# Row mathematics turned on TensorE, merged weight transfers and rows of x for the second block in a pooling and mLSTM layer

## The chip, the core and the metric

The program runs on one core of a Trainium2 chip. The metric is the device time of one execution in microseconds, median of three runs. The engines are named as the profile names them: PE (TensorE), DVE (VectorE), ACT (ScalarE), POOL (GpSimd) and SP (SyncE, whose queue issues all DMAs here).

## What is computed

One layer over x of 2048 tokens with 1024 features: an RMS norm, one input projection, two branches (pooling, and an mLSTM in both directions), a gated merge and an output projection with a second norm.

```python
def hybrid_layer(x, norm_pre_g, w_in, ...):
    h = rms_norm(x, norm_pre_g)          # x * rsqrt(mean(x*x) + EPS) * g
    proj = jnp.einsum('bsd,de->bse', h, w_in)
    u_a, z_a, q, k, v, o, z_b, gates, g_a, g_b = jnp.split(proj, split_points, axis=-1)
    ...                                  # pooling branch: y_a
    q, k = silu(centred_depthwise_conv([q, k])), split again
    ...                                  # gates: i_pre, f_pre, per direction and head
    h_fwd = mlstm_direction(qh, kh, vh, i_pre[0], f_pre[0])
    h_bwd = flip(mlstm_direction(flip(qh), flip(kh), flip(vh), flip(i_pre[1]), flip(f_pre[1])))
    ...                                  # norm, gates: y_b
    merged = sigmoid(g_a + b_merge[0]) * p_a + sigmoid(g_b + b_merge[1]) * p_b
    out = jnp.einsum('bsd,de->bse', merged, w_out)
    return x + rms_norm(out, norm_post_g)

def mlstm_direction(q, k, v, i_pre, f_pre):      # chunks of 128 tokens, 16 of them
    log_f = log_sigmoid(f_pre);  b = cumsum(log_f) in each chunk
    ...
    def step(carry, xs):                          # from chunk to chunk
        m_new = jnp.maximum(bl + m_st, m_add)     # bl, m_add: one number per head and chunk
        ...
```

## The kernel before

Phase 1 is the input projection, and the change lies in it. It treats the tokens in two halves of 1024, each of two blocks of 512, and the columns of w_in in 38 pairs of 128. Each factor is split into an upper part (h) and a rest (l), and a product is three matmuls, h·h, h·l, l·h (`mm3`, L107 to L109). Pairs 0 and 1 of each half are done plainly (`quarters`, L429 to L431); from pair 2 on a Strassen scheme takes sums of the two blocks (S1 to S4, from `combos`) and of the weights (T1 to T4, from `prep_w`, L355 the differences). PSUM banks A, B and C take the products; `u`, `p` and `sg` are what DVE and ACT make of the banks (L398, L403, L746), and a bank's next product waits for that.

The order of the instructions is made by a scheduler from priorities (`high_priority`) and ties (`issue_after`); each engine then runs its list in order. SP's list holds the DMAs, in order too.

**The start** (`operands`, half 0). xT comes as 8 tiles of 512 tokens for each block. For each block, `sums` squares the tiles on ACT (L243), adds the squares on DVE (L245) and sums them over partitions on PE (`ssqp`, L249). `rstd_of` takes the mean on DVE (L154) and the power on POOL (L156), `rows_of` spreads it with four matmuls (`rbp`, L178) and an ACT copy (`rb`, L185). Then DVE scales xT (L197), ACT rounds it (A11h and so on, L95), and DVE or POOL takes the rest (L99). The busy matmuls (L262) only keep PE at work. `sums(1)` is tied behind the second scaled tile of block 0. In `quarters` the order on PE is tied at the last two tiles of block 0 to `rbp` of the block after.

**The weights.** In half 0 `load_w` loads a pair as two tiles `wraw` of 512 KB, `prep_w` makes B11, B21, B22 and T1 to T4, h on ACT and l on POOL or DVE, and `keep_w` (L344) writes the T's to DRAM, h and l in a DMA each. In half 1 `again_w` reads them back (L319, L324, L336). The tiles of both parts come from the pool `wc` with 20 buffers.

**The row mathematics** (`row_math`, half 1). It works on 128 rows (direction, head, chunk) by 128 tokens. After two scans along each row (L853, L854) it takes the last column of each, `ends`, [128, 2], through DRAM (L859) and back as 4 rows of heads with 16 chunks (L864), scans over the chunks (L869), writes the result through DRAM (`carry`, L876) and reads it back as a column (L879). It is a generator: one step is taken in each of the pairs in `ROWS`. Close to it in time are `pair_v`, whose tiles `vnh` and `vnl` have buffers in turn with the conv's `acc` (L655 clears the end of `vnl`, L661 transposes v on PE as `vtr`), and the conv's output DMA `qT<-acc` (L641).

## Time and profile before

| | |
|---|---|
| Median of three runs | 2377.75 us (2377.66 to 2380.99) |
| Profiled execution, device time | 2386.15 us |
| Its span, from first to last instruction | 2384.3 us |
| Mean granted TensorE clock, share of full speed | 0.991 |
| PE busy | 2314.4 us (97%) |
| DVE, ACT, POOL busy | 1466.4 (62%), 900.0 (38%), 1138.0 (48%) us |
| DMA | 521.63 MB, 219 GB/s over the span |

The times of rows are microseconds from the span's start, in the one profiled execution. Busy time of PE says nothing of its clock: a matmul at the lower level counts as busy for twice as long. `[idle <-engine tile line]` behind an instruction is the time its engine stood idle before it, and what ended that.

### The profile page before, as it was taken

To read this page: it belongs to the slowest core of one execution; us is meant where nothing else is said; L and a number is where in the kernel's file an instruction comes from. 1 tells how busy PE (TensorE), PEld (TensorE's weight loads), DVE (VectorE), ACT (ScalarE), POOL (GpSimd) and SP (SyncE) were. 2 spreads that over 40 slices of the span, in tenths; PEclk is the share of its full clock that TensorE was granted. 3 is DMA by queue.
4 is the path that set the end of the run, shared out by engine and by line. 5 is a ranking of instruction groups with operands and counts; after the bars stand their busy time and mean duration, and the time that the engine had idled before them with its cause. 6 is when DMAs were issued, how large, how long until landed. Compare 5 with 4: busy or idle time off the path is not lost.

```text
span 2384.3 us, 35775 instructions
## 1 busy us (share of the span) xinstructions
PE 2314.4 (97%) x12569; PEld 2001.0 (84%) x12569; DVE 1466.4 (62%) x2495; ACT 900.0 (38%) x1773; POOL 1138.0 (48%) x902
## 2 busy tenths in 40 slices
PE   6899999999999989999999999999999999999998
PEld 4688888888888878888888887998989899999786
DVE  6876666677666464455666534888975333354765
ACT  4434433333343423222322333776764111121442
POOL 4655565565545334464564540554565111233775
PEclk9999999999999999999999999999999999999999
DMA  4567656566673566878777876777657546588763
GB/s 138 174 215 276 238 207 230 208 208 223 237 259 137 178 185 201 260 262 273 253 254 244 260 250 245 226 217 234 204 159 233 174 148 207 187 279 283 248 215 124
DMA packets 303011, 521.63 MB, mean 219 GB/s; under 512 B 27504, under 2 KB 138224, under 8 KB 302832
## 3 DMA queue, kind: packets, MB, share of 16 engines
q1 hardware_dynamic: 302832, 519.35, 65.1%
q8 instruction: 99, 1.62, 0.3%
q14 instruction: 80, 0.66, 0.1%
HBM read 318.45 MB, written 200.80 MB: 218 GB/s over the span
## 4 chain that ended last, share of the span: by engine, by line
PE 79%; DVE 7%; DMA 6%; issue 3%; POOL 3%; ACT 2%; SPq 1%; POOLq 0%; DVEq 0%; ACTq 0%
PE bankB L107 8%; PE bankB L108 7%; PE bankB L109 7%; PE bankA L109 5%; PE bankA L108 5%; PE bankA L107 5%; PE bankC L108 5%; PE bankC L107 5%; PE bankC L109 5%; PE num L1232 4%; PE pb L933 2%; PE pb L932 2%; PE pb L934 2%; PE paps L933 2%; PE paps L932 2%
## 5 line engine op out<-in xcount | busy, mean ns | idle before, releaser
L99 POOL TENSOR_TENSOR wB21l<-wraw,wB21h 128x512 fp32r<-128x512 f32 x76 | 106.7, 1405 | 228.3 <-ACT wB21h L95 190.7
L635 DVE SCALAR_TENSOR_TENSOR acc<-raw,conv_w,acc 128x1026 f32<-128x1026 f32 (+1 forms) x96 | 153.8, 1615 | 10.6 <-ACT acc L630 9.7
L99 POOL TENSOR_TENSOR wB22l<-wraw,wB22h 128x512 fp32r<-128x512 f32 x76 | 115.6, 1521 | 87.3 <-ACT wB22h L95 55.2
L1216 POOL TENSOR_TENSOR qs<-q,isc 128x256 f32<-128x256 f32 x120 | 91.2, 762 | 134.2 <-PE num L1232 53.0
L933 PE MATMUL pb<-oxs,w_proj_mlstmh 128*128 128x256 f32 x512 | 144.0, 281 | 0.0
L932 PE MATMUL pb<-oxs,w_proj_mlstmh 128*128 128x256 f32 x512 | 143.6, 281 | 0.0
L934 PE MATMUL pb<-oxs,w_proj_mlstml 128*128 128x256 f32 x512 | 143.4, 280 | 0.0
L933 PE MATMUL paps<-pys,w_proj_poolh 128*128 128x256 f32 x512 | 142.9, 281 | 0.2 <-POOL pys L99 0.2
L932 PE MATMUL paps<-pys,w_proj_poolh 128*128 128x256 f32 x512 | 141.4, 281 | 0.0
L934 PE MATMUL paps<-pys,w_proj_pooll 128*128 128x256 f32 x512 | 141.1, 280 | 0.0
L99 POOL TENSOR_TENSOR wB11l<-wraw,wB11h 128x512 fp32r<-128x512 f32 x72 | 106.9, 1485 | 56.0 <-ACT wB11h L95 52.8
L398 DVE TENSOR_TENSOR u<-bankB,p 128x512 f32<-128x512 f32 x76 | 52.2, 687 | 103.0 <-PE bankB L109 95.8
L107 PE MATMUL bankC<-S1h,wT1h 128*128 128x512 f32 x272 | 106.8, 393 | 3.4 <-ACT sg L746 3.4
L107 PE MATMUL bankB<-S3h,wT3h 128*128 128x512 f32 x272 | 106.8, 393 | 2.3 <-DVE u L398 2.3
L109 PE MATMUL bankB<-S2h,wT2l 128*128 128x512 f32 x272 | 106.2, 390 | 1.3 <-DVE wT2l L99 1.3
L107 PE MATMUL bankB<-A22h,wT4h 128*128 128x512 f32 x272 | 106.1, 390 | 1.3 <-DVE u L403 1.3
L108 PE MATMUL bankB<-S2l,wT2h 128*128 128x512 f32 x272 | 106.9, 393 | 0.0
L107 PE MATMUL bankA<-A12h,wB21h 128*128 128x512 f32 x272 | 106.6, 392 | 0.1
L916 POOL TENSOR_TENSOR nm<-nm,mask 128x256 f32<-128x256 f32 x64 | 61.3, 972 | 95.2 <-DMA nm<-negM 84.6
L108 PE MATMUL bankB<-S3l,wT3h 128*128 128x512 f32 x272 | 106.7, 392 | 0.0
L109 PE MATMUL bankB<-S3h,wT3l 128*128 128x512 f32 x272 | 106.6, 392 | 0.0
L108 PE MATMUL bankC<-S1l,wT1h 128*128 128x512 f32 x272 | 106.5, 392 | 0.0
(443 smaller groups left out, 7729.2 us busy)
## 6 DMA issues: line engine op xcount, KB each, us to landing
wraw<-in_w_in SPq DMA_DIRECT2D x110, 512.0 KB, 4.6
wt<-wT2h SPq DMA_DIRECT2D x34, 256.0 KB, 4.7
wt<-wT1h SPq DMA_DIRECT2D x34, 256.0 KB, 4.4
wt<-wT3h SPq DMA_DIRECT2D x34, 256.0 KB, 3.4
wt<-wT2l SPq DMA_DIRECT2D x34, 256.0 KB, 4.8
wt<-wT1l SPq DMA_DIRECT2D x34, 256.0 KB, 4.0
wt<-wT3l SPq DMA_DIRECT2D x34, 256.0 KB, 2.9
wt<-wT4h SPq DMA_DIRECT2D x34, 256.0 KB, 2.0
```

What stands on the lines that cost most here:

```text
L99: return eng.tensor_tensor(lo, x, hi.bitcast(F32), op=ALU.subtract)
L107: nc.tensor.matmul(ps, wh, xh, start=start and kt == 0, stop=False, skip_group_check=True)
L108: nc.tensor.matmul(ps, wh, xl, start=False, stop=False, skip_group_check=True)
L109: nc.tensor.matmul(ps, wl, xh, start=False, stop=stop and kt == 3, skip_group_check=True)
L398: self.read_banks.append(nc.vector.tensor_tensor(u2, bank["B"], p1, op=ALU.add))
L635: nc.vector.scalar_tensor_tensor(acc[:, :n], raw[:, tap : tap + n], self.cw[:, ct, tap : tap + 1], acc[:, :n], op0=ALU.mult, op1=ALU.add,)
L916: nc.gpsimd.tensor_tensor(t[:, d, :, :], t[:, d, :, :], mask[:, d, None, :].to_broadcast([P, 2, P]), op=ALU.add)
L932: nc.tensor.matmul(ps, wh, xh, start=i == 0, stop=False)
L933: nc.tensor.matmul(ps, wh, xl, start=False, stop=False)
L934: nc.tensor.matmul(ps, wl, xh, start=False, stop=i == n)
L1216: nc.gpsimd.tensor_tensor(qs[d], q[:, :, ck], isc[:, d, j % 2, None, :].to_broadcast([P, 2, P]), op=ALU.mult)
L1232: nc.tensor.matmul(pn, qs[d][:, kt, :], state[:, kt, :], start=kt == 0, stop=False)
```

## The change

The change has three parts.

1. **Start.** xT is stored so that two of its 128-row tiles are one DMA (4 of 512 KB for a block in place of 8 of 256 KB). For the second block of half 0 the sum of squares is taken from rows of x: 8 tiles `xs` of 128 tokens by 512 features, each squared on ACT with the sum over the row as its accumulator (`part`), one DVE add, then `rstd_of` and `rows_of` as before. ssqp and the DVE adds remain for the first block alone. On SP the rows of x stand ahead of the second block's xT. The lower halves of the first weights are made on DVE in place of POOL.
2. **Weights.** h and l of one weight are one tile [128, 2, 4, 128]; `wc` has 10 of them. `keep_w` and `again_w` move both in one DMA of 512 KB (4 in place of 8 for a pair and half). w_in is stored by blocks, so that reading a part of a pair takes runs of 2 KB.
3. **Row mathematics.** `ends` becomes two rows of 128 on one partition by two matmuls (`re`) and an ACT copy; two scans run over 64 numbers of one partition each; two matmuls (`rc`) and an ACT copy give the columns. The DMAs of `ends` and `carry` are gone; the steps are taken in pairs 3, 4, 6, 7 and 9.

```diff
-ROWS = (3, 4, 6, 7, 9, 10)
+ROWS = (3, 4, 6, 7, 9)
...
         def fetch(b):
-            for kt in range(KT):
-                t0 = half * HALF + b * BLK
-                nc.sync.dma_start(X[kt][b], a["xT"][kt, :, t0 : t0 + BLK])
+            for q in range(KT // 2):
+                nc.sync.dma_start(room[b, q], a["xT"][half * 2 + b, :, 2 * q : 2 * q + 2])
...
-            if b == 0:
-                busy(acc[:, :P], acc)
+            busy(X[7][0][:, :P], X[7][0])
...
+        def row_sums():
+
+            self.rows_read = []
+            part = pool.tile([P, 8], F32, tag="ssq", name=self.nm("part"), bufs=2)
+            tiles = []
+            for k in range(8):
+                xs = (pool.tile if k < 5 else self.wt_pool.tile)([P, BLK], F32, tag="p" if k < 5 else "wt", name=self.nm("xs"))
+                r0 = BLK + k % 4 * P
+                self.rows_read.append(nc.sync.dma_start(xs, a["x"][r0 : r0 + P, k // 4 * BLK : (k // 4 + 1) * BLK]))
+                tiles.append(xs)
+            return part, tiles
...
-                last = sums(0)
+                last = sums()
+                part, xs = row_sums()
+                with tc.issue_after(self.rows_read[3].ins):
+                    fetch(1)
...
-                if half == 0 and b == 0 and kt == 2:
-                    with tc.issue_after(scaled[1].ins):
-                        sums(1)
+                if half == 0 and b == 0 and kt == 6:
+                    with tc.issue_after(scaled[5].ins):
+                        assert not xs
+                        nc.vector.tensor_tensor(part[:, :4], part[:, :4], part[:, 4:], op=ALU.add)
+                        self.known = self.rstd_of(part[:, :4], part[:, :4], 0, 1)[0]
+                        self.rows_of(0, 1, rb[:, BLK:], psum)
...
+                if half == 0 and b == 0 and kt > 0:
+                    with tc.issue_after(self.upper.ins):
+                        for _ in range(min(2, len(xs))):
+                            k = 8 - len(xs)
+                            x = xs.pop(0)
+                            nc.scalar.activation(x, x, AF.Square, accum_out=part[:, k : k + 1])
...
+    def parts(self, wc, n):
+
+        t = wc.tile([P, 2, 4, P], F32R, tag="wc", name=self.nm(f"w{n}"))
+        return t, (t[:, 0], t[:, 1])
...
         def kept(n):
-            W[n] = tuple(wc.tile([P, 4, P], F32R, tag="wc", name=self.nm(f"w{n}{p}")) for p in "hl")
-            for p, t in enumerate(W[n]):
-                nc.sync.dma_start(
-                    t.bitcast(F32).rearrange("p k n -> p (k n)"), self.sp[f"wt{i}"][:, self.KEPT.index(n), p, :]
-                )
+            t, W[n] = self.parts(wc, n)
+            nc.sync.dma_start(
+                t.bitcast(F32).rearrange("p a k n -> p a (k n)"), self.sp[f"wt{i}"][:, self.KEPT.index(n)]
+            )
...
-            for p, t in enumerate(W[n]):
-                self.nc.sync.dma_start(self.sp[f"wt{i}"][:, k, p, :], t.bitcast(F32).rearrange("p k n -> p (k n)"))
+            self.nc.sync.dma_start(
+                self.sp[f"wt{i}"][:, k], W[n, "both"].bitcast(F32).rearrange("p a k n -> p a (k n)")
+            )
...
-                if u == 0 and kt == KT - 2 and self.half == 0:
+                if u == 0 and kt == KT - 3 and self.half == 0:
...
-            wc = es.enter_context(tc.tile_pool(name="wc", bufs=20))
+            wc = es.enter_context(tc.tile_pool(name="wc", bufs=10))
...
-                        self.plain_w(W[i], wc, raw[i], 1, "pool")
+                        self.plain_w(W[i], wc, raw[i], 1, "pool" if half else "dve")
...
-        nc.sync.dma_start(self.sp["ends"].rearrange("q r -> r q"), ends)
         yield
-        sc = T(64, NH).rearrange("h (d q c) -> h d q c", d=2, q=2)
...
+        ps = psum.tile([1, 2, P], F32, tag="tr", name="re", bufs=2)
+        for k in range(2):
+            nc.tensor.matmul(ps[:, k, :], ends[:, k : k + 1], self.ident, start=True, stop=True)
+        sc, leaves = T(2 * P, 1).rearrange("o (q r) -> o q r", q=2), one[:1, :]
+        nc.scalar.activation(sc, ps, AF.Copy)
...
+            nc.vector.tensor_tensor_scan(
+                leaves[:, row], sc[:, 0, row], sc[:, 1, row], NEG, op0=ALU.add, op1=ALU.max
+            )
...
         yield
+        ps = psum.tile([P, 2], F32, tag="tr", name="rc", bufs=2)
+        for k, row in enumerate((enters, leaves)):
+            nc.tensor.matmul(ps[:, k : k + 1], row, self.one_c[:1, :], start=True, stop=True)
         mc = T(2)
-        nc.sync.dma_start(mc, self.sp["carry"].rearrange("q r -> r q"))
-        yield
+        nc.scalar.activation(mc, ps, AF.Copy)
...
-        "xT": f(x.T).reshape(KT, P, S),
+        "xT": f(x.T.reshape(KT, P, S // BLK, BLK).transpose(2, 1, 0, 3)),
```

First place, PE in the first block of half 0. Before, the sums of the second block's squares (ssqp) stand in its row:

```order
61 L431 MATMUL bankA_528<-A12l_401,wB21h_483 128x512
62 L429 MATMUL bankB_529<-A12h_400,wB22h_487 128x512
63 L430 MATMUL bankB_529<-A12h_400,wB22l_488 128x512
64 L249 MATMUL ssqp_441<-one_c,sq_438 128x1 x4
65 L431 MATMUL bankB_529<-A12l_401,wB22h_487 128x512
```

Now, at nearly the same place, rbp of the second block (wB_57 and wB_58 are late weights, of pair 1):

```order
57 L462 MATMUL bankB_498<-A12h_401,wB_55_457 128x512
58 L463 MATMUL bankB_498<-A12l_402,wB_55_457 128x512
59 L461 MATMUL bankA_505<-A12h_401,wB_57_462 128x512
60 L461 MATMUL bankB_506<-A12h_401,wB_58_465 128x512
61 L178 MATMUL rbp_442<-ident,rstd 128x128
62 L614 MATMUL gps_513<-A11h_399,wg 32x512
```

The four ssqp are gone, and rbp, which stood at row 78 before, stands at row 61, ahead of the gates' matmuls (gps).

Second place, DVE ahead of pair 2's `u`, in pairs 2 to 4 of half 0. Before (`wt` with two sources is a difference of weights, S4l a rest of the block sums):

```order
76 L99 TENSOR_TENSOR S4l_821<-xT_307,S4h_820 128x512
77 L99 TENSOR_TENSOR S4l_821<-xT_308,S4h_820 128x512
78 L99 TENSOR_TENSOR S4l_821<-xT_310,S4h_820 128x512
79 L99 TENSOR_TENSOR S4l_821<-xT_309,S4h_820 128x512
80 L355 TENSOR_TENSOR wt_864<-wraw_836,wt_844 128x512
...
85 L355 TENSOR_TENSOR wt_985<-wraw_957,wt_965 128x512
86 L355 TENSOR_TENSOR wt_1123<-wraw_1115 128x512
87 L398 TENSOR_TENSOR u_118_913<-bankB_885,p_117_899 128x512
88 L355 TENSOR_TENSOR wt_1125<-wraw_1117,wt_1123 128x512
```

Now:

```order
66 L99 TENSOR_TENSOR S4l_798<-xT_301,S4h_797 128x512 x2
67 L387 TENSOR_TENSOR wt_836<-wraw_813,wt_820 128x512
68 L99 TENSOR_TENSOR S4l_798<-xT_303,S4h_797 128x512 x2
...
73 L387 TENSOR_TENSOR wt_946<-wraw_923,wt_930 128x512
74 L387 TENSOR_TENSOR wt_1077<-wraw_1070 128x512
75 L387 TENSOR_TENSOR wt_1079<-wraw_1072,wt_1077 128x512
76 L430 TENSOR_TENSOR u_100_879<-bankB_851,p_99_865 128x512
77 L387 TENSOR_TENSOR wt_1087<-wraw_1072,wraw_1070 128x512
```

The difference for T4 of pair 2 stands behind two S4l and no longer behind four, and pair 4's second difference (wt_1125, now wt_1079) stands ahead of u and no longer behind it.

Third place, SP in half 1 around the first step of the row mathematics. Before (`acc` is the conv's output; rows are the row mathematics'):

```order
534 L859 DMA ends<-rows 128x2x1
535 L319 DMA wT3h_7301<-wt_95 128x512
536 L319 DMA wT3l_7302<-wt_95 128x512
537 L641 DMA qT_60<-acc_7057 128x1026
538 L336 DMA wraw_7443<-in_w_in 128x4x128
539 L864 DMA rows<-ends 4x2x16
```

Now:

```order
378 L674 DMA qT_60<-acc_6609 128x1026
379 L350 DMA wT_991_6845<-wt_95 128x1024
380 L350 DMA wT_992_6847<-wt_95 128x1024
381 L674 DMA qT_60<-acc_6620 128x1026
382 L367 DMA wraw_6983<-in_w_in 128x512
383 L350 DMA wT_994_6852<-wt_95 128x1024
```

The DMAs of `ends` have gone from between them; the conv's output stands where it stood, behind the reads of the weights, which are one DMA each.

## Rows read from the trace of the kernel before

**Rows 1.** Waits of PE, whole span: releaser, us in total, times, longest.

```profile
PE ssqp L249 <- DVE sq L245: 15.5, 2, 12.3
...
PE vtr L661 <- DVE vnl L99: 7.2, 1, 7.2
```

**Rows 2.** Timeline of PE, start: start us, us, engine line op tile, [idle <-releaser].

```profile
20.74 0.50 PE L429 MATMUL bankA<-A11h,wB11h 128*128 128x512 f32 x1 [1.24 <-ACT A11h L95]
...
24.83 0.50 PE L431 MATMUL bankA<-A11l,wB11h 128*128 128x512 f32 x1 [1.95 <-DVE A11l L99]
...
40.02 1.61 PE L249 MATMUL ssqp<-one_c,sq 128*128 128x1 f32 x8 [3.20 <-DVE sq L245]
```

**Rows 3.** Windows: length; busy of PE, PEld, DVE, ACT, POOL; PEclk, DMA share, GB/s.

```profile
14.00:16.00 2.00, 2.00 (x4) 0.92 (x5) 0.16 (x1) 1.78 (x5) 1.68 (x3) 1.00 1.05 404
...
42.00:44.00 2.00, 2.00 (x6) 1.55 (x5) 0.00 (x0) 0.00 (x0) 0.93 (x1) 0.50 0.00 0
...
46.00:48.00 2.00, 2.00 (x9) 1.45 (x8) 0.00 (x0) 0.00 (x0) 0.00 (x0) 0.73 0.00 0
...
95.00:100.00 5.00, 4.86 (x14) 3.57 (x15) 3.44 (x2) 5.00 (x10) 4.75 (x4) 0.67 0.76 207
...
854.00:856.00 2.00, 2.00 (x11) 1.64 (x10) 0.00 (x0) 0.28 (x1) 0.14 (x1) 1.00 0.21 32
...
866.00:868.00 2.00, 1.54 (x7) 1.54 (x8) 1.00 (x2) 0.39 (x1) 0.00 (x0) 0.50 0.59 179
...
868.00:870.00 2.00, 2.00 (x7) 1.67 (x7) 1.53 (x6) 1.29 (x3) 0.00 (x0) 0.57 0.99 307
```

**Rows 4.** Timeline of DVE, start.

```profile
21.31 1.78 DVE L245 TENSOR_TENSOR sq<-sq,sq 128x512 f32<-128x512 f32 x1
...
34.34 2.45 DVE L197 SCALAR_TENSOR_TENSOR xT<-xT,norm_pre_g,rb 128x512 f32<-128x512 f32 x2
...
50.26 7.47 DVE L197 SCALAR_TENSOR_TENSOR xT<-xT,norm_pre_g,rb 128x512 f32<-128x512 f32 x8 [8.43 <-ACT rb L185]
...
57.65 1.78 DVE L355 TENSOR_TENSOR wt<-wraw 128x512 f32<-128x512 f32 x1
```

**Rows 5.** Instructions that write rstd, on POOL: ns min/median/max, first and last start.

```profile
L156 POOL TENSOR_TENSOR rstd<-ssq,half_c x4: 1006/1021/1484, 14.5 to 216.8; 128x4 f32<-128x4 f32 x4
```

**Rows 6.** Timeline of PE, pairs 2 and 3.

```profile
88.97 0.50 PE L109 MATMUL bankB<-S2h,wT2l 128*128 128x512 f32 x1 [1.32 <-DVE wT2l L99]
...
94.89 0.79 PE L107 MATMUL bankC<-S1h,wT1h 128*128 128x512 f32 x1 [3.37 <-ACT sg L746]
...
104.24 0.50 PE L107 MATMUL bankB<-S3h,wT3h 128*128 128x512 f32 x1 [1.82 <-DVE u L398]
```

**Rows 7.** Timeline of DVE, pairs 2 and 3.

```profile
88.83 3.58 DVE L99 TENSOR_TENSOR S4l<-xT,S4h 128x512 fp32r<-128x512 f32 x4
...
104.43 0.83 DVE L355 TENSOR_TENSOR wt<-wraw,wt 128x512 f32<-128x512 f32 x1 [0.24 <-DMA wraw<-in_w_in]
```

**Rows 8.** Timelines of SP, DVE and PE around the row mathematics.

```profile
847.47 0.37 SPq L859 DMA_DIRECT2D ends<-rows  x1
...
850.70 0.32 SPq L641 DMA_DIRECT2D qT<-acc  x1
...
862.73 0.07 DVE L655 MEMSET vnl<- 128x8 f32 x1 [10.18 <-DMA qT<-acc]
...
863.63 0.18 DVE L869 TENSOR_TENSOR_SCAN rows<-rows 4x16 f32<-4x16 f32 x1 [0.84 <-DMA rows<-ends]
...
866.46 1.97 PE L661 MATMUL vtr<-ident,raw 128*128 128x128 f32 x8 [7.19 <-DVE vnl L99]
```

**Rows 9.** Tile qT, whole span: its DMAs' times from issue to landing.

```profile
DMA to landing us min/median/max: 3.0/5.6/12.0
```

**Rows 10.** Timelines of SP and PE in a pair of half 0.

```profile
307.09 0.33 SPq L344 DMA_DIRECT2D wt<-wT2l  x1
...
325.16 0.39 PE L109 MATMUL bankB<-S2h,wT2l 128*128 128x512 f32 x1
```

More of the change, by code (lines that the diff above doesn't have):

```diff
@@ L94, in split @@
         if hi_eng == "act":
-            nc.scalar.activation(hi, x, AF.Copy)
+            self.upper = nc.scalar.activation(hi, x, AF.Copy)
         else:
@@ L220, in operands @@
         X = {}
-        for kt in range(KT):
-            if kt % 4 == 3:
-                X[kt] = tuple(wc.tile([P, BLK], F32, tag="wc", name=self.nm("xT")) for _ in range(2))
-            else:
-                x = pool.tile([P, HALF], F32, tag="raw" if kt < 4 else "acc", name=self.nm("xT"))
-                X[kt] = x[:, :BLK], x[:, BLK:]
+        room = {}
+        for b, q, where in ((0, 0, "raw"), (0, 2, "acc"), (0, 1, "acc"), (0, 3, "acc"), (1, 0, "raw"), (1, 2, "raw"), (1, 1, wc), (1, 3, wc)):
+            if where is wc:
+                t = wc.tile([P, 2, BLK], F32, tag="wc", name=self.nm("xT"))
+            else:
+                t = pool.tile([P, 2, BLK], F32, tag=where, name=self.nm("xT"))
+            room[b, q] = t
+        for kt in range(KT):
+            X[kt] = tuple(room[b, kt // 2][:, kt % 2] for b in range(2))
         def fetch(b):
-            for kt in range(KT):
-                t0 = half * HALF + b * BLK
-                nc.sync.dma_start(X[kt][b], a["xT"][kt, :, t0 : t0 + BLK])
+            for q in range(KT // 2):
+                nc.sync.dma_start(room[b, q], a["xT"][half * 2 + b, :, 2 * q : 2 * q + 2])
         last = []
@@ L237, in operands, with sums @@
             yield
-            fetch(1)
-        def sums(b):
+            if half == 1:
+                fetch(1)
+        def sums():
             acc = None
@@ L249, in sums @@
                 nc.tensor.matmul(ps[:, i : i + 1], acc[:, i * P : (i + 1) * P], self.one_c, start=True, stop=True)
[L250 to L251 removed]
+            busy(X[7][0][:, :P], X[7][0])
             ssq = pool.tile([P, 4], F32, tag="ssq", name=self.nm("ssq"), bufs=2)
[L253 to L257 removed]
+            ends = self.rstd_of(ssq, ps, 0, 0)
+            self.rows_of(0, 0, rb[:, :BLK], psum)
+            busy(self.rstd[:, :1].to_broadcast([P, P]), X[7][0])
+            return ends
+        def row_sums():
[8 more added lines that the diff above has]
+            return part, tiles
         def busy(w, x):
@@ L333, in again_w @@
         if not self.edge:
-            put("B21", left[:, 4:8, :], "pool")
+            put("B21", left[:, 1], "pool")
         kept("T4")
-        self.read = nc.sync.dma_start(b22, w_in[i, :, 4:8, P:])
+        self.read = nc.sync.dma_start(b22, w_in[i, :, 1, 1])
         put("B22", b22, "pool")
@@ L471, in load @@
                 def load(i):
-                    return [self.load_w(wr, i, slice(4 * j, 4 * j + 4)) for j in range(2)]
+                    return [self.load_w(wr, i, j) for j in range(2)]
                 def work(i, W):
@@ L482, in phase1 @@
                     next(ops)
-                    raw = [self.load_w(wr, i, slice(0, 4)) for i in range(2)]
+                    raw = [self.load_w(wr, i, 0) for i in range(2)]
+                    next(ops)
                     if half == 0:
-                        raw.append(self.load_w(wr, 0, slice(4, 8)))
-                    next(ops)
+                        raw.append(self.load_w(wr, 0, 1))
                     for i in range(2):
-                        self.plain_w(W[i], wc, raw[i], 1, "pool")
+                        self.plain_w(W[i], wc, raw[i], 1, "pool" if half else "dve")
                     next(ops)
@@ new lines, in row_math @@
+        nc.scalar.activation(sc, ps, AF.Copy)
+        chunks = lambda x, d: x[:, d * 64 : (d + 1) * 64].rearrange("o (h c) -> o h c", h=NH)
+        for d, at in enumerate((0, NC_ - 1)):
+            nc.vector.memset(chunks(sc[:, 0, :], d)[:, :, at : at + 1], NEG)
+            row = slice(d * 64, d * 64 + 64) if d == 0 else slice(127, 63, -1)
+            nc.vector.tensor_tensor_scan(
+                leaves[:, row], sc[:, 0, row], sc[:, 1, row], NEG, op0=ALU.add, op1=ALU.max
+            )
+        enters = sc[:, 0, :]
@@ L863, in row_math @@
+        nc.vector.memset(enters, NEG)
         for d in range(2):
-            nc.sync.dma_start(sc[:, d, :, :], src[d])
+            to, of = (slice(1, NC_), slice(0, NC_ - 1)) if d == 0 else (slice(0, NC_ - 1), slice(1, NC_))
+            nc.vector.tensor_copy(chunks(enters, d)[:, :, to], chunks(leaves, d)[:, :, of])
         yield
-        car = T(64, NH).rearrange("h (d q c) -> h d q c", d=2, q=2)
-        nc.vector.memset(car, NEG)
-        for d, st in ((0, 1), (1, -1)):
-            nc.vector.tensor_tensor_scan(
-                car[:, d, 1, ::st], sc[:, d, 0, ::st], sc[:, d, 1, ::st], NEG, op0=ALU.add, op1=ALU.max
-            )
@@ L1551, in layouts @@
     wk = w_in.reshape(KT, P, -1).transpose(1, 0, 2)
-    pair = [np.concatenate([wk[:, :, c0 : c0 + P], wk[:, :, c1 : c1 + P]], axis=2) for _, _, c0, c1 in in_pairs()]
+    pair = [np.stack([wk[:, :, c : c + P].reshape(P, 2, 4, P) for c in cc], axis=2) for _, _, *cc in in_pairs()]
     x = np.asarray(i["x"])[0]
```

46 lines of the change are left out of this document (18 added, 28 removed).

## The prediction

> **What bounds the kernel now.** First the busy shares: PE works 97% of the span and stands idle for about 70 us (2384.3 less 2314.4, in the table above). So an edit of DVE, ACT or the queue is worth only what PE waits for it, plus what a wait does to PE's clock. Then PE's waits over the whole span [rows 1]: the two longest items are the ones this change touches, the sums of squares (15.5 us in two waits, 12.3 of them the start itself) and the transpose of v behind DVE (7.2 us). Then PE's timeline at the start [rows 2] and in pairs 2 and 3 [rows 6], where each wait has its length and its releaser. Last, the windows [rows 3], for the clock: behind such a wait the granted clock is 0.50, the lower of the two levels (1.2 GHz), and what PE does there takes double. I price a stretch at a lower clock as PE's working time in it times (1 less the clock).
>
> The times below come from the profiled execution, 2386.15 us, 8.4 us above the median of 2377.75. I take the sum from the profiled one and subtract the same microseconds from the median.
>
> **The start, up to the second block.** The first matmul starts at 20.74 [rows 2]. Ahead of it the same chain stands: squares, DVE sums, ssqp at 12.3 [rows 1], the power on POOL, rbp, rb, the scaling. The change moves a busy matmul out from between ssqp and rbp and loads the same 2 MB of xT in half as many DMAs; against that, ACT now makes two more weight parts ahead of rb, and DVE four low halves. I put the first matmul at 20.7, with 1.5 us to either side: two ACT parts or two low halves on DVE (0.68 each where POOL rests, 1.78 beside it, [rows 4, 6, 7] show both sizes) come to about that, and a transfer that lands sooner or later by half its share of the 12.3 us can give no more.
>
> The power runs on POOL while DVE now works through the low halves. It took 1.02 us in the median and 1.48 where it took longest [rows 5], so 0.46 us is the price if the two get in each other's way; it lies inside the 1.5.
> The Trainium skill, SBUF — State Buffer, "Who interferes with whom", says of this that a DVE instruction with two SBUF inputs and a GpSimd instruction that reads SBUF exclude each other for the whole instruction. It speaks against moving the lows to DVE at this place; by it the sum below would be 20.3 us in place of 20.8, and the trace's longest power agrees with it without proving it.
>
> Two waits behind it go. At 24.83 PE waits 1.95 us for A11l, because DVE first adds squares of the second block; those adds and their squares are gone, so −1.95. At 40.02 PE waits 3.20 us for the last of these sums, and ssqp's matmuls take 1.61 [rows 2]; none of that is left, since the row sums come out of ACT's accumulator. And the clock falls with that wait: 0.50 from 42 to 46, 0.73 to 48 [rows 3], which is 1.0 + 1.0 + 0.5 lost, with 0.2 between 41.6 and 42: 2.7. Together 7.5, with A11l 9.5 us.
>
> What is late next there? PE needs the second block's rstd (its rbp) only for what follows, but stands in order: it comes now behind 56 matmuls, with the first use of the late weights ahead of it (order, first place). From 24.83 to the wait's start at 36.82 PE did 51 matmuls before (its rows 13 to 63 in the order), 0.235 each, so 56 of them from 20.7 end at 33.9. DVE's last scaling of block 1 ended at 36.79 before (34.34 + 2.45, [rows 4]), with five adds of squares from 21.31 on ahead of it that are gone (the first took 1.78; at 0.7 to 1.8 each 3.5 to 9, I take 5.6), so near 31; then the one small add, the mean and a power of 1.0 to 1.5: rstd near 33, a little ahead of PE. I take no wait there, 1.5 at worst. The rows of x come from 8 DMAs of 256 KB that SP now issues ahead of the second block's four of xT; at the 404 GB/s of the start [rows 3] these 2 MB take 5.2 us, so xT's second block lands about that much later than before, and has until 36. rb of the second block then is ready near 36 (the four rbp, and ACT's copy), and DVE scales it from 36 instead of 50.26 [rows 4]: **DVE is 14 us ahead, PE 9.5.** This order of gains decides the rest of the start.
>
> **Pairs 2 and 3.** From 57.65 on DVE works without a gap until its wT2l at 88.9 and the four S4l behind it [rows 4, 6, 7], so its chain moves as a whole, 14 us earlier.
> - wT2l: PE got it at 88.97 after 1.32 of wait [rows 6]. DVE brings it at 75.0, PE wants it at 88.97 − 1.32 − 9.5 = 78.2. The wait goes: PE is 10.8 ahead.
> - bankC: PE waited 3.37 until 94.89 for a sigmoid on ACT that stands behind wT4's upper half, which waits for a difference on DVE behind four S4l (3.58, [rows 7]). Of these two stand behind it now (order, second place). It is ready at 94.89 − 14 − 1.8 = 79.1, wanted at 94.89 − 3.37 − 10.8 = 80.7. The wait goes, and with it the slow clock: 0.67 from 95 to 100 [rows 3], 5 × 0.33 = 1.65. PE is 15.8 ahead.
> - u: PE waited 1.82 until 104.24 for DVE's u [rows 6]. Wanted after the change at 104.24 − 1.82 − 15.8 = 86.6. DVE brings it 14 us earlier, at 90.2, but one more difference of pair 4's weights now stands ahead of it (order, second place), and this one waited for its weights until 104.43 before [rows 7], that is just behind u. Fourteen earlier it can start at 90.4, 0.83 later u at 91.3, and u itself, about 0.7 like the others of its size, brings PE to about 91.9. So **a new wait of some 5 us takes the place of three old ones**, and of the 15.8 PE keeps 12.4. The clock fell behind the wait of 1.82 as well; I count that part unchanged.
>
> So the start is worth 12.4. At best (the load comes early, u at 86.6) it is 15.8 + 1.8 = 17.6; at worst the late wait is longer and the clock lower for longer, or rbp waits, 8.
>
> **The row mathematics.** PE's one long wait in the second half is 7.2 us for vnl [rows 1]. Followed back: the split that makes vnl stands on DVE behind a MEMSET at 862.73 that waited 10.18 us for the DMA qT<-acc, whose buffer it takes [rows 8]. The DMAs of qT, 16 of the conv's output and 16 more that read it back, take 3.0 us at least, 5.6 in the median and 12.0 at most [rows 9]; issued at 850.70 and waited for until 862.73, this is the longest. It was issued just behind `ends` (847.47, [rows 8]), which writes 128 x 2 single floats, and in the stretch in which both are under way all DMAs together move 32 GB/s [rows 3]. The change makes the turn on PE; `ends` is gone from the queue, qT is not (order, third place). At 5.6 us from its issue qT lands at 856.3. From the MEMSET to vtr on PE 3.7 us passed (862.73 to 866.46), of which 0.84 is DVE's wait for rows<-ends, which goes too [rows 8]; so PE could go on at 856.3 + 2.9 = 859.2, and wanted to at 866.46 - 7.19 = 859.3: no wait, but only just. The clock's part: PE's work from 866.5 to 868 at 0.50 and to 870 at 0.57 [rows 3], 0.75 + 0.86 = 1.6. So −7.2 − 1.6 = **−8.8**, and −5 if qT lands 4 us later than its median.
> What is added: four small matmuls of re and rc, two copies on ACT, scans over one row of 64 on DVE, two of them. No such scan is in the trace; nearest is the old one, 4x16, of 0.18 [rows 8]; 64 steps are four times as many, so 0.18 to 0.72 each, and I take 0.4. Their cover: re's inputs are made on DVE before the MEMSET, and rc stands 84 rows behind re in PE's order, 19 us at 0.235 a matmul. PE itself: four small matmuls, which I take at 0.4 together (ssqp's eight rows took 1.61 [rows 2], at the lower clock). If ACT or DVE were late, rc would make PE wait in order, up to some 3 us.
>
> **The rest.** 34 pairs: weights written and read as one DMA of 512 KB for upper and lower half instead of two of 256 KB, half the weight buffers at double the size, w_in in longer runs. PE does not wait for weights there, and the lead is long: wT2l's write goes out at 307.1, so it is made by then, and PE uses it at 325.2 [rows 10], 18 us later. Cost and gain nothing, ±2 for both halves.
>
> Sum: 12.4 + 8.8 − 0.4 = 20.8. 2386.15 − 20.8 = 2365.3 profiled, **2377.75 − 20.8 = 2357.0** for the median (rounded).
>
> **Rivals.**
> 1. Start and row mathematics both as said: 2357. For it speaks that every removed wait has its releaser by name.
> 2. The row wait stays: qT was slow for another reason (the two reads of 256 KB in front of it, which are 512 KB now), or rc takes its place. Then only the start counts: 2377.75 − 12.4 = 2365. For it: the slack worked out above is 0.1 us. Against: PE waits for vnl nowhere else [rows 1], though qT is written in 16 places.
> 3. The preparation in front of PE binds: DVE, POOL and SP together can't come 14 us earlier, because weights for pairs 2 to 4 arrive as before or rows of x delay the second block's xT. Then DVE comes 6 to 8 us earlier in place of 14, u with it, and the sum is 6 + 8.8: 2363.
> 4. The change doesn't do what it says: the rows of x arrive late, PE waits for rbp instead of for ssqp for as long, and re and rc wait instead of vnl. Within 2 us of before: 2377. Against: the squares of rows need no PE and no DVE add.
> 5. Slower: the writes of a pair's halves as one DMA go out only when the lower half is made, SP stands on them in order, and the loads of the pair after next behind it come late. From a lateness of 18 us [rows 10] PE waits in each of 34 pairs; 1 us each is +34 − 20.8 = +13: 2391. Against: the lead; it decides only when that is used up.
>
> **How the numbers follow.** 1: 0.68. 2: 0.10. 3: 0.10. 4: 0.07. 5: 0.05. The prediction is 1's. Its own range: 17.6 + 8.8 + 2 = 28.4 gives 2349, 8 + 5 − 2 = 11 gives 2367; rivals 2 and 3 lie in it, and with 2 us less for either of their ends it goes from 2347 to 2370. 4 and 5 stay out, 0.12, with a little at the low side. Measurements tell about 0.2%, 4.75 us, from no change; so faster 0.88, same 0.07, slower 0.05.
>
> **What would show it.** Right: no PE wait of over 2 us between 21 and 75; rbp of the second block near 33; the second block's first matmul near 47.7; a wait of 3 to 6 us for u near 91 as the last one of the start; qT<-acc of 4 to 7 us near 837 and no vtr wait. Wrong: a wait at rbp over 2 us, a DVE gap before wT2l, waits of PE for weights between 150 and 800, a wait at rc, or small waits of DVE that stay though PE's have gone.

## The result and the profile after

The changed kernel is faster, by less than forecast. Beside the same runs of before it was measured three times:

| | before, us | changed kernel, us | ratio | 95% interval |
|---|---|---|---|---|
| first comparison | 2378.88 (6 runs) | 2366.28 (6 runs) | 0.9943 | 0.9930 to 0.9956 |
| second (e5) | 2381.54 (11 runs) | 2368.03 (6 runs) | 0.9941 | 0.9927 to 0.9954 |
| third (e9) | 2382.60 (11 runs) | 2368.84 (6 runs) | 0.9941 | 0.9927 to 0.9955 |

That is 12.6 to 13.8 us, where 20.8 were forecast; 2366.3 lies in the range of 2347 to 2370. The profiled executions say something else: 2386.15 before and 2365.91 after, 20.2 us apart and close to the forecast sum. Why these two figures differ is one of the questions below.

The page of the changed kernel, its first lines:

```profile
span 2364.1 us, 35026 instructions
...
PE 2306.9 (98%) x12569; PEld 1994.6 (84%) x12569; DVE 1448.8 (61%) x2495; ACT 901.6 (38%) x1783; POOL 1152.8 (49%) x898
```

PE stands idle for 57 us, not 70. Its waits at the start and, behind the dots, in the stretch with the row mathematics (releaser, us in total, times, longest):

```profile
PE busy L276 <- DMA xT<-in_xT: 9.1, 1, 9.1
PE bankA L107 <- ACT p L424: 2.0, 1, 2.0
PE rbp L178 <- POOL rstd L156: 1.7, 1, 1.7
PE bankC L107 <- ACT sg L779: 1.7, 1, 1.7
PE bankB L107 <- DVE u L430: 1.6, 1, 1.6
PE bankA L107 <- ACT sg L779: 1.1, 1, 1.1
...
PE bankC L107 <- DVE raw L635: 1.2, 1, 1.2
PE vtr L694 <- DVE raw L635: 0.6, 1, 0.6
```

Of the two items of [rows 1] one is gone (vtr for vnl), and of the other nothing is left but its start: a busy matmul now stands ahead of ssqp and waits 9.1 us for xT. PE's timeline at the start, the lines that answer to [rows 2] and [rows 6]:

```profile
19.84 0.50 PE L461 MATMUL bankA<-A11h,wB 128*128 128x512 f32 x1 [0.97 <-ACT A11h L95]
...
32.66 0.38 PE L178 MATMUL rbp<-ident,rstd 128*128 128x128 f32 x2
...
73.19 0.50 PE L109 MATMUL bankA<-A11h,wB 128*128 128x512 f32 x1 [0.73 <-POOL wB L99]
...
80.15 0.50 PE L107 MATMUL bankC<-S1h,wT 128*128 128x512 f32 x1 [1.68 <-ACT sg L779]
...
84.29 0.51 PE L107 MATMUL bankA<-A11h,wB 128*128 128x512 f32 x1 [1.11 <-ACT sg L779]
...
86.84 0.50 PE L107 MATMUL bankA<-A12h,wB 128*128 128x512 f32 x1 [2.05 <-ACT p L424]
...
92.33 0.51 PE L107 MATMUL bankB<-S3h,wT 128*128 128x512 f32 x1 [1.60 <-DVE u L430]
```

Between 19.84 and 73.19 PE waits for nothing: the waits of 1.95 and 3.20 us and the slow clock behind them are gone (one slow stretch of another kind comes in some executions; it is shown under the experiments). From 73.19 on five waits of 0.7 to 2.1 us follow, 7.2 together, and the last is the forecast one, for u. On DVE the answers to [rows 4] and [rows 7]:

```profile
35.75 7.47 DVE L197 SCALAR_TENSOR_TENSOR xT<-xT,norm_pre_g,rb 128x512 f32<-128x512 f32 x8 [4.66 <-ACT rb L185]
...
60.40 0.68 DVE L99 TENSOR_TENSOR S2l<-xT,S2h 128x512 fp32r<-128x512 f32 x1
67.19 1.85 DVE L99 TENSOR_TENSOR S2l<-xT,S2h 128x512 fp32r<-128x512 f32 x1 [6.12 <-ACT S2h L95]
68.97 1.78 DVE L99 TENSOR_TENSOR wT<-wt,wT 128x512 fp32r<-128x512 f32 x1
73.11 3.52 DVE L99 TENSOR_TENSOR S4l<-xT,S4h 128x512 fp32r<-128x512 f32 x2 [2.37 <-ACT S4h L95]
...
90.70 0.98 DVE L387 TENSOR_TENSOR wt<-wraw,wt 128x512 f32<-128x512 f32 x1 [1.94 <-DMA wraw<-in_w_in]
91.60 0.68 DVE L430 TENSOR_TENSOR u<-bankB,p 128x512 f32<-128x512 f32 x1
```

DVE scales the second block from 35.75, 14.5 us earlier, and the difference of pair 4's weights ahead of u waits for its load until 90.70, as the working had it (90.4). What it did not have is the hole in the middle: DVE, which had no gap there before, stands for 6.1 us and again for 2.4. A gap of DVE before wT2l is one of the signs that the prediction names for being wrong. For comparison, the same place before the change:

```profile
87.03 1.28 DVE L99 TENSOR_TENSOR S2l<-xT,S2h 128x512 fp32r<-128x512 f32 x2
88.23 0.68 DVE L99 TENSOR_TENSOR wT2l<-wt,wT2h 128x512 fp32r<-128x512 f32 x1
```

### The profile page after: what moved, and what is told of

It reads as the page before. It is cut to its first block, busy times and chain, and to the rows that moved or that the text cites. A ratio compares the mean times of both kernels' runs of the same rounds, so it can differ in the third digit from the quotient of the medians.

```text
span 2364.1 us, 35026 instructions
## 1 busy us (share of the span) xinstructions
PE 2306.9 (98%) x12569; PEld 1994.6 (84%) x12569; DVE 1448.8 (61%) x2495; ACT 901.6 (38%) x1783; POOL 1152.8 (49%) x898
## 5 line engine op out<-in xcount | busy, mean ns | idle before, releaser
L99 POOL TENSOR_TENSOR wB<-wraw,wB 128x512 fp32r<-128x512 f32 x216 | 324.7, 1506 | 322.8 <-ACT wB L95 245.9
L95 ACT ACTIVATE wB<-wraw 128x512 fp32r<-128x512 f32 x220 | 137.0, 628 | 359.5 <-PE bankB L109 155.3
L99 POOL TENSOR_TENSOR wT<-wt,wT 128x512 fp32r<-128x512 f32 x102 | 150.3, 1475 | 152.2 <-ACT wT L95 128.7
L107 PE MATMUL bankA<-A12h,wB 128*128 128x512 f32 x272 | 107.3, 394 | 2.0 <-ACT p L424 2.0
L107 PE MATMUL bankC<-S1h,wT 128*128 128x512 f32 x272 | 105.9, 389 | 1.7 <-ACT sg L779 1.7
L107 PE MATMUL bankB<-S3h,wT 128*128 128x512 f32 x272 | 105.9, 389 | 1.6 <-DVE u L430 1.6
L107 PE MATMUL bankA<-A11h,wB 128*128 128x512 f32 x272 | 106.3, 391 | 1.1 <-ACT sg L779 1.1
L107 PE MATMUL bankC<-S4h,wB 128*128 128x512 f32 x272 | 106.2, 390 | 1.2 <-DVE raw L635 1.2
L107 PE MATMUL bankB<-A22h,wT 128*128 128x512 f32 x272 | 106.0, 390 | 0.8 <-DVE u L435 0.8
L109 PE MATMUL bankA<-A11h,wB 128*128 128x512 f32 x272 | 105.9, 390 | 0.7 <-POOL wB L99 0.7
L108 PE MATMUL bankB<-S2l,wT 128*128 128x512 f32 x272 | 106.6, 392 | 0.0
L109 PE MATMUL bankA<-A12h,wB 128*128 128x512 f32 x272 | 106.4, 391 | 0.0
```

The source lines that it names most:

```text
L95: self.upper = nc.scalar.activation(hi, x, AF.Copy)
L99: return eng.tensor_tensor(lo, x, hi.bitcast(F32), op=ALU.subtract)
L107: nc.tensor.matmul(ps, wh, xh, start=start and kt == 0, stop=False, skip_group_check=True)
L108: nc.tensor.matmul(ps, wh, xl, start=False, stop=False, skip_group_check=True)
L109: nc.tensor.matmul(ps, wl, xh, start=False, stop=stop and kt == 3, skip_group_check=True)
```

## Experiments

The runs are called e1 to e12, by the numbers in the headings.

**e1: the row mathematics alone, on the kernel before** (the new `row_math` and `ROWS` in the old kernel):

```diff
-ROWS = (3, 4, 6, 7, 9, 10)
+ROWS = (3, 4, 6, 7, 9)
...
-        nc.sync.dma_start(self.sp["ends"].rearrange("q r -> r q"), ends)
...
+            nc.tensor.matmul(ps[:, k, :], ends[:, k : k + 1], self.ident, start=True, stop=True)
```

> The kernel before with the new row mathematics alone (turned on PE, steps in pairs 3, 4, 6, 7, 9; start and weights as before). Theory A, the wait for vnl (7.2 us, with the lower clock behind it 8.8) belongs to the one profiled execution and is not in most executions of before: the timed comparison shows within 2 us of before, whatever the profile shows. Theory B, the wait is in every execution of before and the change takes it away, but something else takes back 8 us: 7 to 9 us faster than before. Both: no vtr wait behind vnl in this profile.

Measured: 2376.31 us beside 2384.50, ratio 0.9970 (0.9958 to 0.9982), 4 to 10 us faster. There is no vtr wait for vnl. Theory A falls: the wait was no accident of one execution.

**e3 and e4: the kernel before, profiled twice more** (no edit).

> The kernel before, profiled a second time. Theory A: the span is 2374 to 2380 and the wait of vtr for vnl is absent or under 2 us, qT written behind ends lands in 3 to 7 us. Theory B: the wait of about 7 us is there again, with qT at about 12 us.

> The kernel before, profiled a third time; the theories expect what they expect of the second profile. Together with it this shows how often the wait for vnl comes, and the other waits at the start (3.2 for ssqp, 3.4 for bankC, 1.8 for u) should come each time.

Spans of 2381.6 and 2380.6 us. The wait is there both times, 5.8 us in place of the 7.2 of [rows 1], behind the same DMA. From the third profile, PE's waits and DVE's timeline:

```profile
PE vtr L661 <- DVE vnl L99: 5.8, 1, 5.8
```

```profile
857.80 0.07 DVE L655 MEMSET vnl<- 128x8 f32 x1 [8.79 <-DMA qT<-acc]
```

So the wait belongs to the program (theory B), and the profile on which the sum was built showed it at its longest.

**e2 and e10: the old row mathematics in the changed kernel**, twice (`row_math`, `ROWS` and the two DRAM tensors of before).

```diff
+ROWS = (3, 4, 6, 7, 9, 10)
...
+        nc.sync.dma_start(self.sp["ends"].rearrange("q r -> r q"), ends)
...
-            nc.tensor.matmul(ps[:, k, :], ends[:, k : k + 1], self.ident, start=True, stop=True)
```

> The changed kernel with the old row mathematics (ends and carry through DRAM, steps in 3, 4, 6, 7, 9, 10). Theory A: as fast as the changed kernel, 11 to 14 us faster than before in the timed runs (ratio near 0.9945); the profile may or may not show a wait of vtr for vnl. Theory B: 3 to 6 us faster than before, with a vtr wait of 6 to 8 us in the profile.

> The changed kernel with the old row mathematics, again, now beside the changed kernel on one chip. If the row mathematics is worth what the added DMA of ends cost (5.5 us) and what it gave alone (7 us): 5 to 7 us slower than the changed kernel, 6 to 10 us faster than before. If the earlier figure holds (13.8 us faster than before): no slower than the changed kernel by more than 2 us, and the two gains don't add.

Measured: 2370.61 beside 2384.50, ratio 0.9942 (0.9930 to 0.9955); and 2371.09 beside 2382.60, 0.9952 (0.9938 to 0.9966), with the changed kernel at 2368.84 on the same chip. So the old way costs the changed kernel 2.3 us there, less than the 5 to 7 expected, and the intervals leave that open. The ratio of e2 is the one that theory A named, not theory B's 3 to 6 us. Yet the wait is in both profiles, at another place: PE waits for `raw`, and DVE, which makes it, for the DMA qT<-acc. PE's waits around it in e10:

```profile
PE vtr L694 <- DVE raw L635: 4.9, 2, 4.3
```

**e6: one DMA more, `ends` written to DRAM in the changed kernel**, read by nothing.

```diff
+        sp["ends"] = self.dram("ends", [2, P])
...
+        nc.sync.dma_start(self.sp["ends"].rearrange("q r -> r q"), ends)
```

> The changed kernel with the one DMA added that writes ends (128 x 2 single floats, 1 KB) to DRAM at its old place; nothing reads it. If these single floats are what holds the other DMAs back: all DMAs together move under 100 GB/s for 8 to 10 us behind it, ends lands after 8 to 10 us, the qT written next lands after 8 to 12 us in place of about 3, PE waits 3 to 7 us near 840 and the time rises by 3 to 8 us. If the reads of 256 or 512 KB in front of qT were the cause: no change of more than 1 us.

Measured: 2373.53 us, and the changed kernel beside it 2368.03: 5.5 us for 1 KB. Windows of this run, columns as in [rows 3], then its DMAs (KB each, median us from issue to landing) and the timelines of DVE and PE:

```profile
834.00:836.00 2.00, 1.85 (x8) 1.54 (x9) 1.97 (x3) 0.00 (x0) 0.63 (x1) 1.00 0.76 41
836.00:838.00 2.00, 2.00 (x11) 1.65 (x10) 1.64 (x2) 0.93 (x1) 0.00 (x0) 1.00 0.76 27
838.00:840.00 2.00, 2.00 (x11) 1.65 (x10) 0.00 (x0) 0.66 (x2) 1.78 (x1) 1.00 0.77 72
840.00:842.00 2.00, 2.00 (x10) 1.65 (x9) 0.00 (x0) 0.00 (x0) 1.87 (x2) 1.00 0.45 39
...
848.00:852.00 4.00, 4.00 (x14) 3.32 (x13) 2.23 (x5) 1.20 (x2) 0.00 (x0) 0.50 0.84 319
```

```profile
wT<-wt SPq DMA_DIRECT2D x4, 512.0 KB, 13.0
qT<-acc SPq DMA_DIRECT2D x2, 513.0 KB, 10.8
...
ends<-rows SPq DMA_DIRECT2D x1, 1.0 KB, 8.9
```

```profile
845.98 0.69 DVE L635 TENSOR_TENSOR raw<-bankB,p 128x512 f32<-128x512 f32 x1 [8.34 <-DMA qT<-acc]
847.41 1.76 PE L694 MATMUL vtr<-ident,raw 128*128 128x128 f32 x7 [4.67 <-DVE raw L635]
```

From 834 to 842, nearly all of it with `ends` under way (issued at 831.5, landed at 840.4), all DMAs together move 27 to 72 GB/s at a busy share of 0.45 to 0.77, and the DMAs issued behind `ends` land late. Without it, in the changed kernel, a window and the same DMAs of the same stretch:

```profile
836.00:838.00 2.00, 2.00 (x10) 1.67 (x9) 0.54 (x1) 0.94 (x2) 1.50 (x1) 1.00 0.59 240
```

```profile
wT<-wt SPq DMA_DIRECT2D x3, 512.0 KB, 5.2
qT<-acc SPq DMA_DIRECT2D x2, 513.0 KB, 3.1
```

Merged reads stand in the queue around qT in both, so they are not the cause. It is shown that the DMA of 256 single floats holds the other DMAs back: DVE waits 8.34 us for qT<-acc, PE 4.7 for DVE's `raw`, and 2.0 are lost at the lower clock (0.50 from 848 to 852).

**e7: upper and lower half in a DMA each**, in the changed kernel (the reads in `again_w` are split in the same way).

```diff
...
-            self.nc.sync.dma_start(
-                self.sp[f"wt{i}"][:, k], W[n, "both"].bitcast(F32).rearrange("p a k n -> p a (k n)")
-            )
+            for p, t in enumerate(W[n]):
+                self.nc.sync.dma_start(self.sp[f"wt{i}"][:, k, p], t.bitcast(F32).rearrange("p k n -> p (k n)"))
```

> The changed kernel with upper and lower half of each T weight written and read in a DMA each (8 of 256 KB in place of 4 of 512 KB for a pair and half); tiles as in the change. I expect no difference from the changed kernel, within 2 us. If the merged DMAs carry a part of the gain: 3 us or more slower than the changed kernel.

Measured: 2363.67 (4 runs) beside the changed kernel's 2368.03 (6 runs): 4.4 us less, against my expectation. Ratios to before 0.9919 (0.9902 to 0.9936) and 0.9941 (0.9927 to 0.9954); the intervals overlap. Its profile (span 2362.8 us) shows little of it: from the first S3T3 to the last gates it takes 697.2 us, where the three profiles of the changed kernel take 697.6. Its start is as long as in the first profile of the changed kernel (S3T3 at 92.4). In the profile of the changed kernel taken beside it (e5) S3T3 comes only at 94.6, for a reason that comes and goes with merged DMAs as well, as the next rows show.

**PE's first matmuls, in e5 and in the first profile of the changed kernel** (no run of its own):

```profile
20.64 0.40 PE L462 MATMUL bankB<-A11h,wB 128*128 128x512 f32 x1
...
32.66 0.38 PE L178 MATMUL rbp<-ident,rstd 128*128 128x128 f32 x2
```

```profile
21.42 0.63 PE L462 MATMUL bankB<-A11h,wB 128*128 128x512 f32 x1
...
34.80 0.38 PE L178 MATMUL rbp<-ident,rstd 128*128 128x128 f32 x2
```

```profile
20.00:40.00 20.00, 20.00 (x83) 15.89 (x84) 12.25 (x19) 11.58 (x28) 10.53 (x8) 1.00 0.52 196
```

The last row is a window of e5, columns as in [rows 3]. Of the others the first lines are the fourth matmul of either, the second ones rbp of the second block. In e5 some nine matmuls from 20 to 24 stand 0.43 us apart, as they do in the kernel before at a granted clock of 0.50 (42 to 46), in place of 0.23; the granted clock is shown as 1.00 in this window all the same, so the rows leave open what holds them up. So rbp comes 2.1 us later, and with it everything up to S3T3. The same slow beginning is in e5, e6, e9, e10 and e11, and not in the first profile, e2, e7, e8 and e12. In the old start the first eight matmuls stand 0.23 apart in all four profiles. What is new ahead of them is that PE stands idle for 1.7 us before rbp of the first block, where a busy matmul filled the time before; no run puts that matmul back, so the cause is not shown.

**e8: the lower part of S1 on DVE.** The hole in DVE's chain ends with ACT's S2h, and that stands behind a weight part that waits 9.1 us for a buffer read by POOL's S1l. On POOL's side the changed kernel shows this (first line its timeline; second all its S1l, ns min/median/max):

```profile
50.98 14.99 POOL L99 TENSOR_TENSOR S1l<-xT,S1h 128x512 fp32r<-128x512 f32 x4 [4.91 <-ACT S1h L95]
```

```profile
L99 POOL TENSOR_TENSOR S1l<-xT,S1h x8: 1282/1292/11245, 51.0 to 775.2; 128x512 fp32r<-128x512 f32 x8
```

One S1l of 11.2 us where the median is 1.3: it stands from 51 until DVE's additions end at 61. In the kernel before the longest is 1.75.

```diff
-        self.put(H, "S1", j, s1, "act", "pool")
+        self.put(H, "S1", j, s1, "act", "dve")
```

> The changed kernel with the lower part of S1 made on DVE instead of POOL (one word in combos). In the profile of the changed kernel POOL's first S1l stands blocked from 51 to 61 us while DVE works through additions, and then DVE waits 6.1 and 2.4 us behind it. If that is what keeps the preparation late: wT2l is ready 4 to 6 us earlier, the five PE waits between 73 and 93 (7.2 us together) fall to under 3, and the time is 3 to 6 us below the changed kernel. If the loads of weights bind, the wait for u stays at 1.5 to 3 us and the gain is 1 to 3.

Measured: 2363.02 us, 5.0 below the changed kernel beside it. But not in the way I expected: S3l now stands blocked in S1l's place, DVE still waits 6.1, wT2l is no earlier (70.6), and two waits on PE are left (5.3 together, for a sigmoid and p). S3T3 comes at 90.6 with no wait for u; it was at 92.3 in the first profile of the changed kernel and at 94.6 in the one beside this, which has the slow beginning. So the edit accounts for 1.8 us in the profile, not for the 5.0. On POOL:

```profile
53.66 14.38 POOL L99 TENSOR_TENSOR S3l<-xT,S3h 128x512 fp32r<-128x512 f32 x4 [7.31 <-ACT S3h L95]
```

**e5 and e9: the changed kernel again, twice.**

> The changed kernel itself, beside the same runs of before as the three below. Theory A (the wait for vnl is in few executions of before): 11 to 14 us faster than before, ratio near 0.9945. Theory B (it is in most, and the row mathematics is worth about 7 us, as e1 and the two new profiles say): where before takes 2380 to 2386 us, 18 to 22 us faster, ratio 0.9915 to 0.9925; the smaller difference measured first then belongs to the level at which before ran there.

> The changed kernel once more, beside the same runs of before as the kernels below. So far it was 12.6 and 13.5 us under before in two comparisons, and 18 to 20 us in pairs of profiles. If the timed figures are right and profiles of single executions scatter by some us: 12 to 16 us again. If the comparison depends on the chip's runs of before (2379 to 2384.5 so far): up to 20 us where before takes over 2384.

Measured: the second and third line of the table at the top. The ratio is the same in all three, whatever the level of before (2378.9 to 2382.6). Of the two outcomes in e9's expectation it is the first. In e5's terms it is theory A's figure, though e1 and the two profiles had shown by then that the wait is real: that the row mathematics is worth its full 7 us on top of the new start does not follow from its being worth that alone.

**e11: the lower parts of S1 and S3 on DVE.**

```diff
-        self.put(H, "S1", j, s1, "act", "pool")
-        self.put(H, "S3", j, s3, "act", "pool")
+        self.put(H, "S1", j, s1, "act", "dve")
+        self.put(H, "S3", j, s3, "act", "dve")
```

> The changed kernel with the lower parts of S1 and of S3 on DVE. With S1 alone there, POOL's first S3l stood blocked in its place (53.7 to 63.1 us) and DVE waited 6.1 us behind it as before. If that block is the cause: DVE has no wait of over 2 us between 36 and 75, wT2l is ready 3 to 4 us earlier than in the changed kernel (67 in place of 71), u 2 to 4 us earlier, and the time is 2 to 5 us below the changed kernel. If POOL's other work or the loads bind: u as in the changed kernel (91.6 to 94) and no gain over 1 us.

Measured: 2362.70 us beside the changed kernel's 2368.84, ratio to before 0.9920 (0.9906 to 0.9935): 6.1 us less, a little over the upper end. DVE's only wait between 45 and 75 is 2.4 us; wT2l is made at 67.7 in place of 71.0 in e9, and PE needs no wait for u:

```profile
67.67 0.68 DVE L99 TENSOR_TENSOR wT<-wt,wT 128x512 fp32r<-128x512 f32 x1
68.27 0.68 DVE L99 TENSOR_TENSOR S2l<-xT,S2h 128x512 fp32r<-128x512 f32 x1
71.38 1.76 DVE L387 TENSOR_TENSOR wt<-wraw,wt 128x512 f32<-128x512 f32 x1 [2.43 <-POOL wT L99]
```

```profile
89.07 0.51 PE L107 MATMUL bankB<-S3h,wT 128*128 128x512 f32 x1
```

That is 5.3 us earlier than in e9 (94.34), which has the slow beginning too, and most of the 6.1.

**e12: the same with two DMAs**, e11's edit and e7's.

> The kernel of e11 with upper and lower half of each T weight in a DMA each, as in e7. The run e7 was 4.4 us under the changed kernel, though its profile shows nothing of that behind 95 us. If the merged DMAs cost something: 3 to 5 us below e11. If that was scatter: within 2 us of e11.

Measured: 2359.65 us (5 runs), ratio to before 0.9907 (0.9891 to 0.9923): 3.0 below e11, at the low end of what a cost of the merged DMAs would give. It is the fastest kernel here, 22.9 us under before and 9.2 under the changed kernel, measured on one chip. Twice, in different kernels, the split came out 3 to 4 us faster; each time the intervals overlap. In this profile (span 2362.5 us) S3T3 comes 1.1 us earlier than in e11, which had the slow beginning where this one has not, and the stretch from there to the gates takes 697.0 us where the merged DMAs take 697.6 to 699.5; the rest is as long or longer. That the merged DMAs cost 3 to 4 us is possible, not shown: a rival is that the two kernels differed by chance in how often PE began slowly.

## Why the prediction was right in kind and too large

To see which term was off, I cut the profiled executions at three marks: the first matmul of S3T3 in pair 2 (end of the start), the last gates' matmul with A22h in half 1, and the first num of the mLSTM. The row mathematics lies between the last two. In us:

| | executions | to S3T3 | gates to num |
|---|---|---|---|
| old start | 4 (before three times, e1) | 101.8 to 104.2, mean 103.2 | |
| new start | 7 (changed three times, e2, e6, e7, e10) | 92.3 to 94.6, mean 93.5 | |
| `ends` through DRAM, old start | 3 (before) | | 691.6 to 693.8, mean 692.8 |
| `ends` through DRAM, new start | 2 (e2, e10) | | 691.7 and 692.3 |
| `ends` written besides, new start | 1 (e6) | | 697.4 |
| rows on PE | 8 (changed three times, e1, e7, e8, e11, e12) | | 684.9 to 687.1, mean 686.3 |

From S3T3 to the gates, and from num to the end, the means of before and of the changed kernel agree within 1.5 us, which is less than single executions differ there. So in the profiles the two named terms are the whole effect: 9.6 + 6.5 = 16.1 us. How the parts of the start (rows of x, larger DMAs of xT, low halves on DVE) share the 9.6 no run separates.

- **First matmul** (20.7 ± 1.5): 19.8 to 20.3 in the seven profiles. Right. The power took 1.41 us beside DVE's low halves, and 1.52 for the second block, against 1.02 in the median before: 0.4 and 0.5 us, about the 0.46 allowed. That agrees with the rule of the Trainium skill, SBUF — State Buffer, "Who interferes with whom", which the prediction cites.

```profile
13.62 1.41 POOL L156 TENSOR_TENSOR rstd<-ssq,half_c 128x4 f32<-128x4 f32 x1 [13.18 <-DVE ssq L154]
...
30.24 1.52 POOL L156 TENSOR_TENSOR rstd<-part,half_c 128x4 f32<-128x4 f32 x1 [0.30 <-DVE part L154]
```

- **Squares, ssqp and the clock** (7.5 and 1.95): the waits went as said. rbp of the second block runs from 32.7 on without a wait, and DVE starts the second block at 35.75 (forecast 36). But this is so in three of the seven profiles with the new start; in the four with the slow beginning rbp comes at 34.4 to 34.8 and DVE's second block at 37.5 to 37.9. The prediction gave PE's first matmuls a time to start and no clock.
- **DVE's chain moves as a whole**: wrong in its working. DVE starts the second block 14.5 us ahead and runs through its additions in 0.6 us steps where it took up to 1.78 beside POOL, so that at its third S2l (60.4, before 87.0) it is 26.6 ahead. Then it loses 6.1 and 2.4 us behind POOL's blocked S1l. wT2l starts at 69.0 and is done at 70.8, forecast 75; u is only 11.9 ahead, for it waits for the load.
- **One wait of 5 us for u in place of three**: PE waits five times, 7.2 us together, for POOL's weight part, twice sg, p and u. S3T3 stands at 92.3 (forecast 91.9). S3T3 held because the load of weights in front of u set the end, as the working said, and not because every step in between was right: that DVE came earlier than forecast and five waits came instead, and that the two left S3T3 in its place, is luck. With the S1l and S3l moved (e11) it is 89.1.
- **The start's 12.4** measured 9.6 over the executions. 104.24 in [rows 6] is the latest of the four profiles with the old start, 1.1 us behind their mean. On the other side, S3T3 comes at 92.3 to 92.6 where PE begins at full pace (forecast 91.9) and at 94.1 to 94.6 with the slow beginning; four of seven with it take another 1.1 from the mean.
- **The row mathematics' 8.8, less 0.4** measured 6.5. The mechanism was right to the DMA: qT lands in 3.1 us, vnl is no longer waited for, re, rc and the two scans on a row (0.46 together) hold up nobody. Off was the size: the wait was 7.2 in the profile used, and 5.8 in both others. And a new wait of about 1.1 us (for `raw`, near 832) came near it; it is in every profile with the new start, also in e2 and e10, so the new row mathematics did not bring it. On the old start (e1) the stretch is 7.9 us shorter than in before's mean, on the new one 5.4 (means of the changed kernel and of e2 and e10).
- **The rest, ±2**: in the profiles the merged DMAs cost about 0.5 us, between S3T3 and the gates; the timed runs of e7 and e12 came out 3 to 4 us faster without them, with intervals that overlap.

So the mechanism was right in the main, and the sizes were not. Two steps of the prediction made the sum 4.7 us larger than these 16.1.

The first is its second paragraph: *I take the sum from the profiled one and subtract the same microseconds from the median.* The profiled execution stood 8.4 us above that median of three; it is 3.9 above the median of the 39 timed runs of before (2382.2, from 2376 to 2388), and the three runs lay 4.5 below that. Its wait for vnl is the longest and its S3T3 the latest that any profile of before shows: 0.9 and 1.1 us of the 4.7. The second is what was put at nothing: a slow beginning of PE (1.1 in the mean) and a new wait in front of the row mathematics (1.1). The remaining 0.5 is S3T3 at 92.4 in place of 91.9.

That the two profiled executions first compared lie 20.2 us apart, close to the forecast sum, is luck in part: the one before has the latest S3T3 and the longest wait of its kind, the one after has no slow beginning, and 1.1 us of the 20.2 lie between S3T3 and the gates, where the change does nothing that the other profiles show.

Sized by the means over the profiles, 16.1, the median would have been 2361.6. Between 16.1 and the 12.6 to 13.8 timed some 2 to 3 us stay open: the three profiled executions of before average 2384.0, 1.8 above the median of the 39 timed ones, which covers part of it, and each comparison carries about 3 us to either side.

How the two gains add is not settled to better than that either. Timed, the row mathematics gives 4 to 10 us alone (e1) and 2.3 on top of the new start (e10 and e9), and the `ends` DMA costs 5.5 (e6). In the profiles the same three are 7.9, 5.4 and 10.8 us in the stretch from the gates to num.

The rivals: the row wait did not stay (2); the preparation did come earlier (3); a time of no change (4) and slower weights that cost the kernel its gain (5) did not occur. Rival 5's place, the merged weight DMAs, is where 3 to 4 us may have gone, though the profiles show only about 0.5 of it.

## What to carry to other kernels

Price a stall from more than one profiled execution, and where only one is there, see first how far it stands from the median: the longest waits of a slow execution are not what the median pays. A chain that "moves as a whole" moves only as far as the engine it shares something with; look for that engine's first instruction in the new order. A small DMA of single floats is dear for what it does to the transfers behind it; here PE turned the two columns in 0.6 us (re) and ACT copied them in 0.36. And when two profiles of a kernel differ, look first for a stretch in which PE's matmuls stand twice as far apart, before the edit is given the credit.
